# Two conformers ahead of the delta rule's groups, and twelve small copies on another engine

## The chip, the cores and the metric

The kernel runs on one core of one Trainium2 chip. The metric is the device time of one execution in microseconds. The core has TensorE (PE: matrix products into PSUM), VectorE (DVE), ScalarE (ACT), GpSimd (POOL), and SyncE (SP), whose queue issues the DMAs of this kernel. Each engine takes its instructions strictly in the order in which they were put on it.

## The reference, cut to what matters

One layer of a hybrid encoder, for a prompt of 2048 tokens and a decode group of 32 tokens that share all weights. Three mixers read the same normalised input, and their outputs are joined:

```python
hn = rmsnorm(h, W['norm_mix'][i])
proj = hn @ W['w_in'][i]
qkv_pre, z, ba, u5, cc = jnp.split(proj, [OFF_Z, OFF_BA, OFF_S5, OFF_CC], axis=-1)
ya, ... = gdn_mixer(...)        # conv of width 4 on q/k/v, then the chunked delta rule
yb, ... = s5_mixer(u5, ...)     # diagonal state space model, scan over time, GLU
yc, ... = conformer_conv(cc, ...)
mix = jnp.concatenate([ya, yb, yc], axis=-1)
h = h + mix @ W['w_out'][i]
hf = rmsnorm(h, W['norm_ffn'][i])
h = h + (silu(hf @ W['ffn_w1'][i]) * (hf @ W['ffn_w3'][i])) @ W['ffn_w2'][i]
h = h + (p[i] @ W['pe_w'][i]) * sigmoid(h @ W['pe_gate_w'][i])
```

`conformer_conv` is a gate, a causal depthwise convolution of width 31 over 256 channels, a LayerNorm and a swish. It needs nothing but its own columns of the projection and the 30 tokens before. `gdn_mixer` convolves q, k and v over four tokens, and then carries a matrix state from chunk to chunk: block b needs the state that block b-1 leaves. `s5_mixer` carries a state too. All is fp32 at the interface; each large product is made of three products of split operands (high x high, low x high, high x low).

## The kernel before, in words

The tokens are in four blocks of 512 columns (`BLK`; the last block has the 32 decode tokens too, 544 columns in two chunks of 272). Features are on the 128 partitions. Two phases run over the blocks:

- `PhaseA.block(b)`, b = 0 to 3: the projection. `conv` makes one of the 12 column groups of q, k and v: it loads a weight, puts the last three columns of the block before (`tails`, for the decode group `taild`) in front of the tile `raw`, writes the product behind them on VectorE (L615), keeps the new last three columns in `tails`, and then either convolves (blocks 0 and 1) or stores `raw` to DRAM as it is (blocks 2 and 3, `G.raw`, L620). `raw` has two buffers. The small copies are those of lines 609, 611, 616 and 618.
- `PhaseF.block(b)`: output projection `w_out` on the mixers' outputs `mixT[b]` (loaded in L1155, split into `fah` and `fal`), the FFN (`hidden` and `w2`, in groups of four hidden tiles and a last one of two), the gated embedding, the final norm. Products go to PSUM tiles `ps_d` (three buffers, `psD`), and VectorE takes them out: L1173 for w_out, L1218 for w2, L1242 and L1243 for the gates.

Beside them runs the mixers' work that isn't a plain product, written as Python generators ("heads"): `s5_init`, `conformer_block(b)`, `gdn_group` (two per block, and one for the decode group after block 3) and `s5_unit(u)` (two, of two blocks each). A `yield k` gives k steps back. Each call of `dense` counts its columns, and whenever a stage's number of columns is reached (`STAGE`: 9216 in PhaseF's block 0, else 7168), every running generator goes on by one step. So the heads' instructions are emitted in between the dense ones. `first_heads` (s5_init, conformer 0, gdn 0) and `first_s5` run beside PhaseA; `later_heads` starts with PhaseF and makes, in this order, conformer 1, gdn 1, conformer 2, s5 1, gdn 2, conformer 3, gdn 3. Before `PhaseF.block(b)` the heads are emitted at least as far as gdn b.

The order on each engine is then made by a scheduler that works with a simulated time: among the instructions that are ready it takes the one of the lowest priority number. Weight loads, splits and evictions have the class "first"; the heads and the dense matmuls have the class "later", in the order of their emission. An instruction of the heads can thus run long before the place where it was emitted, where an engine is free.

The heads' memory is a stack on the right side of SBUF: `R(name)` opens a pool, and a pool that is opened after another was closed lies in the same place; a tile there waits for the tiles before it that it overlaps (`reuse_waits="tile"`). Conformer 1's pool `cc_1` follows the pool of S5's first unit; gdn 1's pool lies over `cc_1`; conformer 2's over gdn 1's, and so on.

In `conformer_block` the taps are L824 (the first of 31) and L826 (30 more), for two halves of 128 channels: 62 instructions on VectorE for a block. Then come transposes on TensorE (L837), statistics (L840, L841), transposes back (L856) and the swish (L864).

Of the kernel before, what the change touches and what calls it, by code (L numbers as in the profile page):

```python
# [18 lines left out]
BLK = 512  # L19
# [15 lines left out]
def chunks_of(n):  # L35
    c = -(-n // 512)
    w = n // c
    return [(i * w, w) for i in range(c)]


def pieces(c0, cn, hist):

    out = []
    a, b = c0, min(c0 + cn, BLK)
    if a < b:
        out.append((0, hist + a, b - a))
    a, b = max(c0, BLK), c0 + cn
    if a < b:
        out.append((a - c0, hist + BLK + hist + (a - BLK), b - a))
    return out  # L50
# [30 lines left out]
def load_weight(G, src, K, name, key):  # L81


    nc = G.nc
    shp = [P] + (list(K) if isinstance(K, tuple) else [K]) + [P]
    with G.first():
        wr = G.wraw.tile(shp, F32, tag="wr", name=f"wr_{name}")
        nc.sync.dma_start(wr, src)
        wh = G.whi.tile(shp, F32R, tag="wh", name=f"wh_{name}")
        wl = G.wlo.tile(shp, F32R, tag="wl", name=f"wl_{name}")  # L90
        kept = G.low.get((name, key))
        if kept is not None:
            nc.sync.dma_start(wl.bitcast(F32), kept)
        nc.scalar.activation(wh, wr, AF.Copy)  # L94
        if kept is None:

            e = nc.vector if name == "w3" else nc.gpsimd
            e.tensor_tensor(wl, wr, wh.bitcast(F32), op=ALU.subtract)  # L98
            if G.NB > 1:
                kept = G.dd.tile(shp, F32, tag=f"lo_{name}{key}", name=f"lo_{name}{key}")  # L100
                G.low[(name, key)] = kept
                nc.sync.dma_start(kept, wl.bitcast(F32))
    return wh, wl


def dense(G, pool, tag, w, xh, xl, ks, c0, cn, start=True, stop=True, ps=None):

    nc = G.nc
    wh, wl = w
    if ps is None:  # L110
        ps = pool.tile([P, 512], F32, tag=tag, name="ps_d")
    K = len(ks)
    G.step(3 * K * cn)
    with G.later():
        _dense(nc, ps, wh, wl, xh, xl, ks, K, c0, cn, start, stop)
    return ps
# [455 lines left out]
class PhaseA:  # L572
# [27 lines left out]
    def conv(self, m, jj, b, hf, hl, bc, n, last, t0):  # L600

        G, A, wp = self.G, self.A, self.wp
        nc = G.nc
        V = nc.vector
        tails, taild, cw = self.tails, self.taild, self.cw
        w = load_weight(G, A.w_in[m], KD, "qkv", m)
        W = BLK + (3 + TS if last else 0)
        raw = wp.tile([P, W + 3], F32, tag="raw", name="raw")
        nc.gpsimd.tensor_copy(raw[:, 0:3], tails[:, m])
        if last:  # L610
            nc.gpsimd.tensor_copy(raw[:, BLK + 3:BLK + 6], taild[:, m])
        for c0, cn in chunks_of(n):
            p_ = dense(G, G.psD, "pd", w, hf, hl, list(range(KD)), c0, cn)
            for so, do, ln in pieces(c0, cn, 3):
                V.tensor_tensor(raw[:, do:do + ln], p_[:, so:so + ln], bc[:, c0 + so:c0 + so + ln], op=ALU.mult)  # L615
        nc.gpsimd.tensor_copy(tails[:, m], raw[:, BLK:BLK + 3])
        if last:
            nc.gpsimd.tensor_copy(taild[:, m], raw[:, W:W + 3])
        if b in G.raw:
            nc.sync.dma_start(G.sild[b][:, jj], raw)  # L620
            return
        acc = wp.tile([P, W], F32, tag="gacc", name="gacc")
        nc.scalar.activation(acc, raw[:, 0:W], AF.Copy, scale=cw[:, m, 0:1])
        for t in range(1, 4):
            V.scalar_tensor_tensor(acc, raw[:, t:t + W], cw[:, m, t:t + 1], acc, op0=ALU.mult, op1=ALU.add)
        th = wp.tile([P, W], F32, tag="gth", name="gth", bufs=1)
        nc.scalar.activation(th, acc, AF.Tanh)
        V.scalar_tensor_tensor(acc, th, 1.0, acc, op0=ALU.add, op1=ALU.mult)
        nc.sync.dma_start(G.sild[b][:, jj, 0:BLK], acc[:, 0:BLK])
        if last:  # L630
            nc.sync.dma_start(G.sild[b][:, jj, BLK:BLK + TS], acc[:, BLK + 3:W])
# [626 lines left out]
def trunk_kernel(ctx: ExitStack, tc: tile.TileContext, A):  # L1258
    nc = tc.nc
# [51 lines left out]
    NB = G.NB  # L1311
# [60 lines left out]
    R = lambda name, bufs=1: tc.tile_pool(name=name, bufs=bufs, side="right", reuse_waits="tile")  # L1372

    def conf(b, wp):
        return conformer_block(G, A, b, wp, G.psM)
# [13 lines left out]
    def conf_of(b):  # L1389
        with R(f"cc_{b}") as wp:  # L1390
            yield from conf(b, wp)

    def s5_of(u):
        with R(f"s5_{u}") as wp:
            yield from s5_unit(G, A, u, wp, G.psM)

    def gdn_of(b):
        with R(f"gd_{b}", 2) as sp:
            for i in range(2):
                state[0] = yield from gdn_part(b, i, state[0], sp)  # L1400
# [37 lines left out]
    ready = [0]  # L1438

    def later_heads():  # L1440
        for b in range(1, NB):
            yield from conf_of(b)
            if b % G.UB == 0:
                yield from s5_of(b // G.UB)
            yield from gdn_of(b)
            ready[0] = b

    G.start(later_heads())
    for b in range(NB):
        G.flush(lambda: ready[0] >= b)  # L1450
# [117 lines left out]
```

## Time and profile before

| what | value |
|---|---|
| median of three runs | 2888.64 us (2888.06 to 2892.27) |
| the profiled execution | 2888.11 us |
| its span (first to last instruction) | 2886.3 us |
| TensorE busy | 2763.9 us, 96% of the span |
| TensorE weight load busy | 2359.9 us, 82% |
| VectorE busy | 1751.6 us, 61% |
| ScalarE busy | 935.2 us, 32% |
| GpSimd busy | 549.4 us, 19% |
| PhaseF's blocks start at | 682.7, 1230.75, 1779.3 and 2347.25 us |

The start of a block of PhaseF is its first matmul with `wh_out`. In the profile's rows "busy" is the time in which an engine executes; a row with "<-" names in brackets how long the engine was idle before the instruction and what ended the idle time. A row of stretches gives, for each engine, busy time and number of instructions, then TensorE's granted clock (1.00 is full speed), the DMA engines' share and GB/s.

### The profile page before, as it was taken

Reading aid. Unit: us, or ns where it says so; the run is one execution under the profiler, and the core shown is the slowest. Engines: PE = TensorE matmul, PEld = TensorE weight load, DVE = VectorE, ACT = ScalarE, POOL = GpSimd, SP = SyncE. Lnnn points to the kernel's source line nnn. Section 1 sums busy time; section 2 is a strip of 40 time slices with the busy share of each in tenths; the row PEclk is TensorE's granted clock in tenths of the full one; section 3 lists DMA queues with packets and bytes.
Section 4 is the critical chain, followed back from the end, with each engine's and each line's share of the span. In section 5 each row is a group of like instructions: output and inputs, shape, how many; then the busy total and the mean of one; then the engine's idle time right before and its main releaser. Section 6 shows DMA issues by size and latency. Waiting matters only on the chain.

```text
span 2886.3 us, 41015 instructions
## 1 busy us (share of the span) xinstructions
PE 2763.9 (96%) x15300; PEld 2359.9 (82%) x15300; DVE 1751.6 (61%) x3933; ACT 935.2 (32%) x1409; POOL 549.4 (19%) x460
## 2 busy tenths in 40 slices
PE   7899999999999999899999999999999979999997
PEld 5668778898878887688888887778888869999997
DVE  8969765865675847966563755856464733333343
ACT  4243423313422222343422333342332423222232
POOL 5731312234232323421010101000010110000000
PEclk9999999999999999999999999999999979999998
DMA  6578777657654555487665657566565654555553
GB/s 225 170 252 269 248 227 227 199 181 245 206 185 167 190 168 200 152 288 220 216 183 176 187 174 242 187 207 192 172 193 154 197 193 149 174 175 176 175 187 107
DMA packets 278919, 565.32 MB, mean 196 GB/s; under 512 B 67344, under 2 KB 126880, under 8 KB 278576
## 3 DMA queue, kind: packets, MB, share of 16 engines
q1 hardware_dynamic: 278720, 562.70, 60.4%
q8 instruction: 121, 1.98, 0.3%
q14 instruction: 78, 0.64, 0.1%
HBM read 457.76 MB, written 104.25 MB: 195 GB/s over the span
## 4 chain that ended last, share of the span: by engine, by line
PE 64%; DVE 8%; DMA 3%; issue 3%; SPq 1%; ACT 1%; POOL 0%; DVEq 0%; POOLq 0%; ACTq 0%
PE ps_d L122 57%; DVE cacc L826 3%; PE ps_kk L935 1%; PE ps_q L1013 1%; PE ps_z L1026 1%; DVE ct L982 1%; DVE cx L983 1%; DVE hb L1218 1%; DMA xd<-cx 1%; DMA hb<-mixT 1%; PE ps_vn L1069 0%; PE ps_o L1083 0%; PE ps_o L1084 0%; PE ps_s L1076 0%; PE ps_ks L1056 0%
## 5 line engine op out<-in xcount | busy, mean ns | idle before, releaser
L94 ACT ACTIVATE wh_w<-wr_w 128x1024 fp32r<-128x1024 f32 (+1 forms) x272 | 281.3, 1034 | 762.9 <-PE ps_d L122 551.4
L122 PE MATMUL ps_d<-fah,wh_w 128*128 128x512 f32 (+1 forms) x1760 | 379.4, 354 | 7.4 <-DVE fa L1196 2.9
L122 PE MATMUL ps_d<-fal,wh_w 128*128 128x512 f32 (+1 forms) x1760 | 376.5, 353 | 0.0
L122 PE MATMUL ps_d<-fah,wl_w 128*128 128x512 f32 (+1 forms) x1760 | 376.1, 353 | 0.0
L122 PEld LDWEIGHTS ps_d<-fah,wh_w 128*128 128x128 f32 x1760 | 291.1, 189 | 53.6 <-issue 4.0
L122 PEld LDWEIGHTS ps_d<-fal,wh_w 128*128 128x128 f32 x1760 | 291.4, 189 | 43.2
L122 PEld LDWEIGHTS ps_d<-fah,wl_w 128*128 128x128 f32 x1760 | 291.3, 189 | 43.2 <-issue 0.4
L1218 DVE TENSOR_TENSOR hb<-hb,ps_d 128x512 f32<-128x512 f32 (+1 forms) x240 | 139.7, 583 | 167.1 <-PE ps_d L122 166.7
L122 PE MATMUL ps_d<-acth,wh_w 128*128 128x512 f32 (+1 forms) x880 | 210.3, 355 | 9.1 <-DVE hb L1218 7.7
L122 PE MATMUL ps_d<-acth,wl_w 128*128 128x512 f32 (+1 forms) x880 | 210.1, 354 | 0.0
L122 PE MATMUL ps_d<-actl,wh_w 128*128 128x512 f32 (+1 forms) x880 | 208.6, 354 | 0.0
L826 DVE SCALAR_TENSOR_TENSOR cacc<-xc,cc_w,cacc 128x512 f32<-128x512 f32 (+1 forms) x240 | 189.4, 824 | 0.0
L122 PEld LDWEIGHTS ps_d<-acth,wh_w 128*128 128x128 f32 x880 | 148.6, 189 | 34.7 <-DVE hb L1218 6.1
L122 PEld LDWEIGHTS ps_d<-actl,wh_w 128*128 128x128 f32 x880 | 149.4, 189 | 22.2
L122 PEld LDWEIGHTS ps_d<-acth,wl_w 128*128 128x128 f32 x880 | 149.2, 189 | 22.2
L98 POOL TENSOR_TENSOR wl_w<-wr_w,wh_w 128x1024 fp32r<-128x1024 f32 (+1 forms) x46 | 108.2, 2351 | 253.9 <-ACT wh_w L94 226.3
L1201 DVE SCALAR_TENSOR_TENSOR fth<-ps_d,bc 128x512 f32<-128x512 f32 (+1 forms) x110 | 64.8, 589 | 132.0 <-PE ps_d L122 131.3
L1196 DVE TENSOR_TENSOR fa<-ps_d,bc 128x512 f32<-128x512 f32 (+1 forms) x110 | 64.5, 588 | 118.5 <-PE ps_d L122 109.4
L122 PE MATMUL ps_d<-hh,wh_qkv 128*128 128x512 f32 (+1 forms) x480 | 107.2, 365 | 13.8 <-DVE raw L615 13.0
L1204 DVE TENSOR_TENSOR actl<-fa,acth 128x512 fp32r<-128x512 f32 (+1 forms) x110 | 81.3, 739 | 51.3 <-ACT acth L1203 50.9
L1199 DVE SCALAR_TENSOR_TENSOR fa<-fth,fa 128x512 f32<-128x512 f32 (+1 forms) x110 | 73.1, 667 | 58.8 <-ACT fth L1198 58.6
L122 PE MATMUL ps_d<-hh,wl_qkv 128*128 128x512 f32 (+1 forms) x480 | 105.5, 361 | 2.3 <-POOL wl_qkv L98 2.3
(479 smaller groups left out, 4783.3 us busy)
## 6 DMA issues: line engine op xcount, KB each, us to landing
wr_w<-in_w SPq DMA_DIRECT2D x256, 512.0 KB, 4.3
wl_w<-lo_w SPq DMA_DIRECT2D x192, 512.0 KB, 4.0
lo_w<-wl_w SPq DMA_DIRECT2D x64, 512.0 KB, 2.9
wr_qkv<-in_w_in SPq DMA_DIRECT2D x48, 512.0 KB, 4.7
wl_qkv<-lo_qkv SPq DMA_DIRECT2D x36, 512.0 KB, 4.2
wr_out<-in_w_out SPq DMA_DIRECT2D x32, 512.0 KB, 5.2
wr_gate<-in_pe_gate SPq DMA_DIRECT2D x32, 512.0 KB, 4.3
wl_out<-lo_out SPq DMA_DIRECT2D x24, 512.0 KB, 5.9
```

The source lines that it names most:

```text
L94: nc.scalar.activation(wh, wr, AF.Copy)
L98: e.tensor_tensor(wl, wr, wh.bitcast(F32), op=ALU.subtract)
L122: nc.tensor.matmul(ps[:, :cn], a[:, i, :], x(k)[:, c0:c0 + cn], start=start and p_ == 0 and i == 0, stop=stop and p_ == 2 and i == K - 1)
L826: V.scalar_tensor_tensor(acc[:, j], xc[:, j, t:t + W], cn_.w[:, j, t:t + 1], acc[:, j], op0=ALU.mult, op1=ALU.add)
L935: nc.tensor.matmul(kk4[:, h - h0], kq[:, 2 * h, cw], kq[:, 2 * h:2 * h + 2, cw], start=True, stop=True)
L982: V.tensor_tensor(t, cx[:, 0:nq, j:j + 1].to_broadcast(sh), cu[:, j:j + 1, j + 1:].to_broadcast(sh), op=ALU.mult)
L983: V.tensor_tensor(cx[:, 0:nq, j + 1:], cx[:, 0:nq, j + 1:], t, op=ALU.subtract)
L1196: V.tensor_tensor(a, p1[:, :cn], bc[:, cs], op=ALU.mult)
L1199: V.scalar_tensor_tensor(a, th, 1.0, a, op0=ALU.add, op1=ALU.mult)
L1201: V.scalar_tensor_tensor(th, p3[:, :cn], 0.5, bc[:, cs], op0=ALU.mult, op1=ALU.mult)
L1204: V.tensor_tensor(fb[:, cs], a, fa[:, cs].bitcast(F32), op=ALU.subtract)
L1218: V.tensor_tensor(hb[m][:, c0:c0 + cn], hb[m][:, c0:c0 + cn], p_[:, :cn], op=ALU.add)
```

## The change

Two edits. The four copies of `conv` are made on VectorE instead of GpSimd: 12 column groups in four blocks with two copies each, and in the last block two more each, 120 copies of 128x3. And `later_heads` opens the pools of conformers 1 and 2 side by side and makes both conformers first; the rest follows in the same order as before: gdn 1, s5 1, gdn 2, conformer 3, gdn 3.

```diff
         raw = wp.tile([P, W + 3], F32, tag="raw", name="raw")
-        nc.gpsimd.tensor_copy(raw[:, 0:3], tails[:, m])
+        V.tensor_copy(raw[:, 0:3], tails[:, m])
         if last:
-            nc.gpsimd.tensor_copy(raw[:, BLK + 3:BLK + 6], taild[:, m])
+            V.tensor_copy(raw[:, BLK + 3:BLK + 6], taild[:, m])
         ...
-        nc.gpsimd.tensor_copy(tails[:, m], raw[:, BLK:BLK + 3])
+        V.tensor_copy(tails[:, m], raw[:, BLK:BLK + 3])
         if last:
-            nc.gpsimd.tensor_copy(taild[:, m], raw[:, W:W + 3])
+            V.tensor_copy(taild[:, m], raw[:, W:W + 3])
 ...
     def later_heads():
+
+        first = list(range(1, min(3, NB)))
+        with ExitStack() as cx2:
+            wps = [cx2.enter_context(R(f"cc_{b}")) for b in first]
+            for b, wp in zip(first, wps):
+                yield from conf(b, wp)
         for b in range(1, NB):
-            yield from conf_of(b)
+            if b not in first:
+                yield from conf_of(b)
             if b % G.UB == 0:
                 yield from s5_of(b // G.UB)
             yield from gdn_of(b)
```

## The prediction

> **What bounds the kernel now.** I read the page first (engines, slices), then the waits of TensorE by stretches, then the timeline at the four places where it idles, and last the chain of waits there.
>
> ```profile
> PE 2763.9 (96%) x15300; PEld 2359.9 (82%) x15300; DVE 1751.6 (61%) x3933; ACT 935.2 (32%) x1409; POOL 549.4 (19%) x460
> PE   7899999999999999899999999999999979999997
> DVE  8969765865675847966563755856464733333343
> PEclk9999999999999999999999999999999979999998
> ```
>
> TensorE is busy 96% of a span of 2886.3 us; the 122 us that are left lie in few slices: the first two, slice 17 (about 1155 to 1227 us), slice 33 (2309 to 2381) and the last. Only there can a change of order gain. Names: F0 to F3 are the four blocks of PhaseF, "heads" the work of the generator chain. The stretches of F0, F1, F2 and of the gap before F3, with each engine's busy time (PE, PEld, DVE, ACT, POOL) and TensorE's clock:
>
> ```profile
> 682.00:1231.00 549.00, 528.85 (x2495) 429.90 (x2494) 378.61 (x627) 172.28 (x248) 189.85 (x95) 0.99 0.57 191
> 1231.00:1776.00 545.00, 543.68 (x2688) 448.07 (x2686) 317.69 (x768) 189.13 (x275) 59.88 (x46) 1.00 0.64 201
> 1776.00:2316.00 540.00, 528.36 (x2529) 432.30 (x2528) 341.45 (x813) 189.30 (x289) 44.98 (x36) 0.99 0.62 196
> 2316.00:2354.00 38.00, 18.02 (x71) 12.68 (x72) 17.13 (x32) 8.68 (x14) 10.63 (x8) 0.56 0.50 174
> ```
>
> Who TensorE waited for in 1120 to 1210 us (first three rows: total, times, longest), and in 2310 to 2350 (last three):
>
> ```profile
> PE ps_d L122 <- DVE hb L1218: 10.0, 6, 3.0
> PE ps_d L122 <- ACT gth L1241: 3.9, 3, 3.0
> PE ps_d L122 <- ACT wh_w L94: 1.2, 1, 1.2
> ...
> PE ps_ot L1109 <- DVE o L1101: 10.1, 1, 10.1
> PE ps_d L122 <- ACT fah L1134: 5.7, 1, 5.7
> PE ps_vn L1069 <- DMA X<-xd: 4.4, 1, 4.4
> ```
>
> The first group is F0's tail, where w2's last group has only six matmuls to an eviction (L1218) while conformer 2's 62 taps sit between the evictions on VectorE. The second is the end of gdn(3), its short decode part, which F3 waits for. The 240 taps of L826 are four conformers; those of conformer 1 (60 of them, 500 to 660 us) and of conformer 2 (1080 to 1230):
>
> ```profile
> 500.00:660.00 160.00, 42.10 (x60) 0.99 0.61 192
> 1080.00:1230.00 150.00, 58.75 (x60) 0.97 0.52 180
> ```
>
> That is 0.70 us a tap early and 0.98 late. The heads' order, by their marks in the timeline (gdn(1)'s last output, conformer 2's last, s5(1)'s first load, F2's first matmuls (two rows), gdn(3)'s last output, F3's first matmuls):
>
> ```profile
> 1108.89 0.75 DVE L1110 SCALAR_TENSOR_TENSOR zy<-ps_ot,gnw,zy 128x512 f32<-128x512 f32 x1 [4.74 <-DMA zy<-zgd]
> 1237.06 0.68 DVE L864 SCALAR_TENSOR_TENSOR cxn<-cth,cxn 128x512 f32<-128x512 f32 x1
> 1244.37 0.43 SPq L438 DMA_DIRECT2D glu<-in_glu_w  x1
> 1779.32 0.50 PE L122 MATMUL ps_d<-fah,wh_out 128*128 128x512 f32 x1 [3.16 <-ACT fah L1134]
> 1780.59 1.66 PE L122 MATMUL ps_d<-fah,wh_out 128*128 128x512 f32 x3 [0.78 <-ACT fah L1134]
> 2341.55 0.35 DVE L1110 SCALAR_TENSOR_TENSOR zy<-ps_ot,gnw,zy 128x128 f32<-128x128 f32 x1 [0.72 <-PE ps_ot L1109]
> 2347.25 2.94 PE L122 MATMUL ps_d<-fah,wh_out 128*128 128x272 f32 x9 [5.74 <-ACT fah L1134]
> ```
>
> Are the heads late because they are emitted late, or because each step waits for the one before? Counted from the yields, a conformer has 18 steps, gdn(1) 64, s5 48, gdn(2) 80, and gdn(3) with its decode part 108: the end is step 354. F0 emits 112 steps (1,032,192 columns by 9216), F1 and F2 144 each (by 7168). Step 354 stands at step 98 of F2, at 1776 + 98 x 540/144 = 2143 us; it ran at 2341.6. So from s5(1) on the heads are bound by their own latency, and what s5(1) starts earlier the end gains one for one, until F2's dense work is the later of the two. The chain of waits at the end shows it:
>
> ```profile
> 2316.27 1.83 DMA xd<-cx
> 2318.24 1.69 DMA X<-xd
> 2319.97 1.47 PE ps_vn L1069 x8
> ```
>
> **The change part by part.** Durations are from the profiled execution: 2888.11 us, of which 2886.3 are the span; the median of the three runs is 2888.64, so one scale serves.
>
> *Conformer 2 leaves F0's tail.* Its taps, statistics and output move; their number, their DMAs (one load, two stores on SP's queue) stay. The 15.1 us of TensorE's waits above have it as cause, since it is every second instruction on VectorE there; gdn(1)'s last steps now run in this stretch instead and keep a few. Ends 0 and -20 (15.1 and some 5 of reduced clock: 0.97 over 150 us); I take -12.
>
> *It goes to 617 us and on,* behind conformer 1's taps, which ran from 563 to 617 in phase A's last block (its first and last instruction, then the stretch):
>
> ```profile
> 563.17 0.55 DVE L824 TENSOR_SCALAR cacc<-xc,cc_w,cc_b 128x512 f32<-128x512 f32 x1 [0.81 <-DMA xc<-xcd]
> 616.75 0.73 DVE L826 SCALAR_TENSOR_TENSOR cacc<-xc,cc_w,cacc 128x512 f32<-128x512 f32 x1
> ...
> 560.00:682.00 122.00, 119.63 (x968) 117.91 (x967) 80.04 (x197) 26.14 (x44) 32.74 (x49) 0.99 0.60 192
> ```
>
> VectorE is 80.0 of 122 us busy there, with conformer 1 in it; 62 taps at 0.70 are 43 us, so they fill the rest and run on into F0's w_out. Cover for the evictions: three PSUM buffers. No cover for gdn(0): its end is on the path to F0, as these rows show (its last output, the load of it on SP, F0's first matmul):
>
> ```profile
> 674.32 0.75 DVE L1110 SCALAR_TENSOR_TENSOR zy<-ps_ot,gnw,zy 128x512 f32<-128x512 f32 x1
> 677.47 0.84 SPq L1155 DMA_DIRECT2D hb<-mixT  x2
> 682.70 0.74 PE L122 MATMUL ps_d<-fah,wh_out 128*128 128x512 f32 x2 [0.21 <-ACT fah L1134]
> ```
>
> What taps do to such a chain: gdn(0)'s 31 solve steps among conformer 1's taps took 52 us, gdn(2)'s, alone, 22.
>
> ```profile
> L983 DVE TENSOR_TENSOR cx<-cx,ct x31: 153/194/220, 542.3 to 594.6; 128x60 f32<-128x60 f32 x3, 128x28 f32<-128x28 f32 x2, 128x54 f32<-128x54 f32 x2, 128x48 f32<-128x48 f32 x2
> L983 DVE TENSOR_TENSOR cx<-cx,ct x31: 171/211/240, 1486.3 to 1508.1; 128x60 f32<-128x60 f32 x3, 128x28 f32<-128x28 f32 x2, 128x54 f32<-128x54 f32 x2, 128x48 f32<-128x48 f32 x2
> ```
>
> So 30 us over 62 dependent instructions, 0.5 us each. From 617 to 675 gdn(0) has some 20 dependent ones: 10 us, by which F0 starts later. Ends 0 (all taps sink into gaps) and 43 (all ahead); I take +10, near the per-instruction row.
>
> A rule against this: the Trainium skill, GPSIMD Engine Reference, section Specifications, says that GpSimd's SBUF interfaces are shared with VectorE and contend with VectorE instructions of two SBUF inputs, which the taps are. The late taps at 0.98 fit it: GpSimd is 35% busy in F0 (189.85 of 549), 27% in the early stretch (32.74 of 122). If the new place were as bad, F0 would slip by 14 instead of 10 and the sum be 4 worse; conformer 1's 0.70 was measured in the new place itself, so the sum keeps it.
>
> *gdn(1) is emitted 18 steps later,* s5(1) at the same place. A step of F0 is 9216 columns; at full clock 577 matmuls of 272 columns fill 72.2 us:
>
> ```profile
> 2525.50:2597.70 72.20, 72.20 (x577) 72.20 (x576) 24.60 (x56) 18.62 (x29) 0.00 (x0) 1.00 0.55 175
> ```
>
> so a step is 4.2 us and 18 are 76. With the slip, gdn(1) ends at 1109 + 76 + 10 = 1195 instead of 1109; F0 ends at 1231 - 12 + 10 = 1229, 34 us later, so F1 doesn't wait. Behind gdn(1)'s end stand, on SP, F1's eight loads and then s5(1)'s first load: about 12 us, 1207. Before it was 1244, because conformer 2 stood between and held its memory until 1237. The heads are 37 us earlier from here.
>
> *F2's start.* gdn(2) ends 37 us earlier, F1 only 2; the 3.9 us for `fah` at F2's start (3.16 and a second of 0.78) go: -4. Late next is conformer 3, which moves into F1's last gates: it costs there what it cost in F2's w_out, so 0.
>
> *F3's start.* gdn(3) ends at 2341.6 - 37 = 2305. F2's dense work ended at 2316; it ends at 2316 - 12 + 10 - 4 + 4 = 2314, the last 4 for gdn(3)'s matmuls, which now lie inside. Output, load and split after 2305 took 5.7 us (2341.55 to 2347.25), so they are through at 2311. F3 starts near 2315, not 2347. In the sum, apart from the shifts: F3's first 22 matmuls were through at 2354 and need 2.8 us at full clock, so some 35 us lay between F2's and them; 31 of these go. Ends 0 (heads no earlier) and -31. I take -31.
>
> *The copies.* 120 copies of 128x3 leave GpSimd for VectorE. GpSimd's and VectorE's nearest rows, what GpSimd's copies waited for, and what TensorE waited for up to 655 us:
>
> ```profile
> L609 POOL COPY raw<-tails x48: 183/232/2390, 62.3 to 640.3; 128x3 f32<-128x3 f32 x48
> L493 DVE COPY X<-s5x 64x2 f32<-64x2 f32 x16 | 2.6, 161 | 0.2
> ...
> POOL raw L609 <- DMA sild<-raw: 55.2, 19, 5.7
> ...
> PE ps_d L122 <- DVE raw L615: 15.0, 7, 5.8
> PE ps_d L122 <- POOL wl_qkv L98: 2.3, 1, 2.3
> ```
>
> 120 x 0.16 = 19 us of VectorE work over phase A; 24 of them (4 us) in block 0, where VectorE is full (slice 2: 9). Against that, GpSimd's queue no longer stands in front of `wl_qkv`. No row shows a copy waiting on VectorE. Ends -17 (both waits of TensorE go) and +55 (every wait for a buffer moves over and reaches TensorE); I take +3, near block 0's 4.
>
> Sum: -12 + 10 - 4 + 4 - 31 + 3 = -30; 2888.1 - 30 = 2858 us.
>
> **The rivals.** (B) *The heads gain nothing.* If conformer 2 takes its whole old stretch in the new place (1108.9 to 1237.1: 128 us instead of 86), gdn(1) ends at 1237, s5(1) starts as before, F3 starts at gdn(3)'s end as before, and the stalls saved earlier are only waited out there: 2887. For it: it shares VectorE and two PSUM buffers with gdn(0). Against: at F0's start VectorE has room for 18 steps.
>
> (C) *VectorE takes over GpSimd's waits.* VectorE runs in order; a copy that waits for `sild<-raw` (up to 5.7 us) holds the evictions behind it. All 55.2 us on the path: 2858 + 55 = 2913; from 30 us on the change is no gain, from 36 it is slower. Against: the eviction into the same buffer has the same wait, only later, and TensorE has three PSUM buffers.
>
> (D) *Relief.* GpSimd free, block 0's 17 us go, and gdn(0) isn't held up: 2858 - 17 - 3 - 10 = 2828 at best, likelier 2836.
>
> (E) *Half.* The heads come only 15 us earlier: F3 starts at 2332; 2873.
>
> **How the numbers follow.** Forecast 0.52 (2838 to 2875), E 0.07, D 0.10, B 0.14, C 0.17. A measurement of this kernel can tell 0.2%, 5.8 us. Faster 0.52 + 0.07 + 0.10 = 0.69; same 0.14; slower 0.17. Range 2836 to 2894: it takes in B and the beginning of C, leaves out half of D and most of C, under 2 in 10.
>
> **What would show it.** Right: conformer 2's taps near 0.7 us between 600 and 700; the waits on `hb` L1218 in F0's tail under 5 us; s5(1)'s first load near 1207; F3's first matmul within 5 us of F2's last; F0's first matmul near 693. Wrong: s5(1) at 1235 or later (B), TensorE waiting for L615 in blocks 2 and 3 of phase A (C), F1 waiting for `fah` at its start, or conformer 3 among w2's last evictions in F1 as conformer 2 was in F0.

## Result and profile after: 1.8% slower

The changed kernel takes 2941.82 us (median of 4 runs, 2940.84 to 2943.91) against 2889.18 us of the kernel before, run beside it: ratio 1.0182, 95% interval 1.0167 to 1.0198. Forecast were 2858 us and a range of 2836 to 2894. The profiled execution has a span of 2941.7 us. Its page, in the lines that the prediction read first (busy time; TensorE's busy tenths in 40 slices of 73.5 us; its granted clock):

```profile
PE 2775.5 (94%) x15300; PEld 2370.6 (81%) x15300; DVE 1756.1 (60%) x4053; ACT 938.8 (32%) x1409; POOL 494.6 (17%) x340
PE   7789899996799999999999999999999979999997
PEclk9899999996899999999999999999999979999998
```

VectorE and GpSimd did what the diff says: 120 instructions moved, VectorE 4.5 us more, GpSimd 54.8 less. TensorE has a hole that wasn't there (slices 10 and 11 from the left: 6 and 7, clock 0.6 and 0.8), its dip in F0's tail (slice 17 before) is gone, and the dip ahead of F3 has stayed. The stretches of the changed kernel, cut at the first matmul of F0, F1, F2 and F3, columns as in the prediction (length, then busy time and count of PE, PEld, DVE, ACT, POOL, then clock, DMA share, GB/s):

```profile
0.00:761.40 761.40, 650.83 (x3514) 538.80 (x3514) 575.61 (x1503) 237.91 (x376) 183.94 (x159) 0.92 0.64 203
761.40:1285.00 523.60, 520.68 (x2482) 427.70 (x2483) 323.93 (x554) 165.80 (x232) 181.19 (x87) 1.00 0.58 193
1285.00:1832.00 547.00, 544.93 (x2668) 449.70 (x2668) 311.10 (x750) 189.65 (x276) 57.52 (x43) 0.99 0.65 203
1832.00:2401.00 569.00, 540.88 (x2577) 439.39 (x2575) 352.29 (x838) 190.42 (x291) 54.85 (x41) 0.97 0.60 189
2401.00:2941.70 540.70, 518.18 (x4062) 515.00 (x4062) 193.16 (x410) 155.03 (x236) 17.08 (x12) 0.97 0.51 168
```

And of the kernel before, the first stretch:

```profile
0.00:683.00 683.00, 634.55 (x3487) 528.59 (x3488) 508.78 (x1291) 226.55 (x359) 231.35 (x267) 0.97 0.69 220
```

Before, the other four were 548, 548, 568 and 539 us long (the starts in the table of the profile before). So the account is short: phase A is 78 us longer (62 of them idle TensorE; 16 more busy, with 27 matmul records more, conformer 2's transposes, and a mean clock of 0.92 against 0.97), F0 is 24 us shorter, the rest is as it was. What F0 waited for, in the timeline of the changed kernel (gdn(0)'s last output, F0's first loads of it, F0's first matmul; then gdn(1)'s last output, s5(1)'s first load, gdn(3)'s last output, F3's first matmul):

```profile
754.47 0.75 DVE L1110 SCALAR_TENSOR_TENSOR zy<-ps_ot,gnw,zy 128x512 f32<-128x512 f32 x1 [5.52 <-DMA zy<-zgd]
757.89 2.23 SPq L1155 DMA_DIRECT2D hb<-mixT  x5
761.44 4.25 PE L122 MATMUL ps_d<-fah,wh_out 128*128 128x512 f32 x9 [12.43 <-ACT fah L1134]
...
1254.39 0.75 DVE L1110 SCALAR_TENSOR_TENSOR zy<-ps_ot,gnw,zy 128x512 f32<-128x512 f32 x1 [0.34 <-DMA zy<-zgd]
1266.89 0.33 SPq L438 DMA_DIRECT2D glu<-in_glu_w  x1
...
2393.98 0.34 DVE L1110 SCALAR_TENSOR_TENSOR zy<-ps_ot,gnw,zy 128x128 f32<-128x128 f32 x1
2401.49 1.78 PE L122 MATMUL ps_d<-fah,wh_out 128*128 128x272 f32 x6 [13.33 <-ACT fah L1134]
```

F0 waits for gdn(0), whose last output comes at 754 instead of 674. The solve of its second half, which took 52 us before (542.3 to 594.6), in the changed kernel:

```profile
L983 DVE TENSOR_TENSOR cx<-cx,ct x31: 176/207/224, 581.7 to 702.5; 128x60 f32<-128x60 f32 x3, 128x28 f32<-128x28 f32 x2, 128x54 f32<-128x54 f32 x2, 128x48 f32<-128x48 f32 x2
```

It begins 39 us late and takes 121 us. Each instruction is nearly as short as before (mean 207 ns against 194); what is new stands between the steps. Two questions follow: which edit makes gdn(0) late, and why nothing is won before F3.

### The profile page after: what moved, and what is told of

It is laid out like the page before. It is cut to its first block, busy times and chain, and to the rows that moved or that the text cites. A ratio compares the mean times of both kernels' runs of the same rounds, so it can differ in the third digit from the quotient of the medians.

```text
span 2941.7 us, 40924 instructions
## 1 busy us (share of the span) xinstructions
PE 2775.5 (94%) x15300; PEld 2370.6 (81%) x15300; DVE 1756.1 (60%) x4053; ACT 938.8 (32%) x1409; POOL 494.6 (17%) x340
## 4 chain that ended last, share of the span: by engine, by line
PE 73%; DVE 14%; DMA 7%; issue 3%; SPq 2%; ACT 1%; POOL 1%; DVEq 0%; ACTq 0%; POOLq 0%
PE ps_d L122 65%; DVE cacc L826 3%; DVE gacc L625 1%; DMA wl_qkv<-lo_qkv 1%; PE ps_kk L935 1%; PE ps_q L1013 1%; PE ps_z L1026 1%; DMA hb<-mixT 1%; DMA mixT<-zy 1%; DVE kq L891 0%; PE ps_o L1083 0%; DVE hb L1253 0%; PE ps_ks L1056 0%; PE ps_o L1084 0%; PE ps_s L1076 0%
## 5 line engine op out<-in xcount | busy, mean ns | idle before, releaser
L1218 DVE TENSOR_TENSOR hb<-hb,ps_d 128x512 f32<-128x512 f32 (+1 forms) x240 | 139.8, 584 | 190.7 <-PE ps_d L122 190.3
L826 DVE SCALAR_TENSOR_TENSOR cacc<-xc,cc_w,cacc 128x512 f32<-128x512 f32 (+1 forms) x240 | 184.8, 800 | 0.0
L98 POOL TENSOR_TENSOR wl_w<-wr_w,wh_w 128x1024 fp32r<-128x1024 f32 (+1 forms) x46 | 107.8, 2344 | 254.0 <-ACT wh_w L94 236.8
L1204 DVE TENSOR_TENSOR actl<-fa,acth 128x512 fp32r<-128x512 f32 (+1 forms) x110 | 87.9, 799 | 44.1 <-ACT acth L1203 43.9
```

What stands on the lines that cost most here:

```text
L826: V.scalar_tensor_tensor(acc[:, j], xc[:, j, t:t + W], cn_.w[:, j, t:t + 1], acc[:, j], op0=ALU.mult, op1=ALU.add)
L1204: V.tensor_tensor(fb[:, cs], a, fa[:, cs].bitcast(F32), op=ALU.subtract)
L1218: V.tensor_tensor(hb[m][:, c0:c0 + cn], hb[m][:, c0:c0 + cn], p_[:, :cn], op=ALU.add)
```

## The experiments

Each kernel was timed beside the kernel before on the same chip. One kernel's runs lie up to 19 us apart, so the ratios decide; a stretch comes from one profiled execution each, and a difference of a few us in it says nothing. "Setup" is `s5_init`'s part on TensorE (L340 to L368: eight transposes with each of two inputs, and 32 small products), the first work of the heads that TensorE does; S5's unit 0, conformer 0 and gdn(0) come behind it.

### Each edit alone

`copies_only` has the diff's first part, `order_only` its second.

> The kernel before with the copies of the short convolution's history on VectorE and nothing else. Theory 1 (the order alone costs the 52 us): 2888 +- 6 us, conformer 0's first tap near 226 us as before, gdn(0)'s last output near 674. Theory 2 (the copies alone make the heads 36 us late in phase A, and the order only passes this on): conformer 0's first tap near 252, gdn(0)'s second solve from about 580, its last output near 705, F0 starts 25 to 35 us late, 2905 to 2920 us. Theory 3 (both are needed: the copies bring the lateness, which costs nothing until conformer 2's taps are ready beside the late solve): the marks of theory 2 in phase A, and a time under 2915.

> The kernel before with conformers 1 and 2 first and nothing else. Theory 1: gdn(0)'s second solve starts near 542 us as before, conformer 2's taps stand between its steps from about 560 on and it takes 100 us or more instead of 52; F0's first matmul near 740 to 760; 2925 to 2945 us. Theory 2: the solve is through before conformer 2's taps are ready, F0's first matmul by 700, 2855 to 2880 us, as forecast. Theory 3: in between, F0's first matmul 700 to 740, 2880 to 2925.

Measured: copies alone 2933.44 us, ratio 1.0146 (1.0127 to 1.0165); order alone 2883.74 us, 0.9983 (0.9971 to 0.9995). Theory 1 falls: the order alone costs nothing, the copies cost nearly all. Of theory 2 the early marks came (251 and 580 us), but the copies alone cost more than it allowed (F0 40 us late, a time above 2920); with the order alone F0 starts at 705, the in-between of theory 3. The stretches of the kernel with the order alone up to F2's end:

```profile
0.00:705.00 705.00, 638.15 (x3514) 529.45 (x3514) 551.94 (x1383) 236.96 (x376) 252.86 (x278) 0.96 0.68 219
705.00:1227.00 522.00, 519.49 (x2480) 427.85 (x2481) 323.16 (x554) 165.78 (x233) 180.41 (x87) 1.00 0.58 194
1227.00:1776.00 549.00, 545.80 (x2669) 449.63 (x2668) 311.97 (x750) 189.75 (x277) 57.28 (x44) 0.99 0.64 203
1776.00:2344.00 568.00, 540.71 (x2579) 440.95 (x2578) 353.33 (x840) 191.26 (x292) 52.91 (x41) 0.97 0.59 190
```

The order gains 26 us in F0 and loses 22 ahead of it. With the copies alone (first two stretches) it is 40 us ahead of F0 and nothing behind:

```profile
0.00:723.00 723.00, 641.60 (x3498) 533.12 (x3498) 526.96 (x1426) 233.25 (x368) 181.40 (x154) 0.94 0.66 212
723.00:1269.00 546.00, 528.42 (x2478) 431.08 (x2479) 375.14 (x610) 167.87 (x238) 183.52 (x88) 0.98 0.55 186
```

Both together give 761.4: the order costs 38 us ahead of F0 when the copies have made gdn(0) late, 22 when they haven't. The same row of gdn(0)'s solve, with the order alone:

```profile
L983 DVE TENSOR_TENSOR cx<-cx,ct x31: 153/196/222, 541.5 to 619.7; 128x60 f32<-128x60 f32 x3, 128x28 f32<-128x28 f32 x2, 128x54 f32<-128x54 f32 x2, 128x48 f32<-128x48 f32 x2
```

78 us, between 52 and 121: conformer 2's taps start at 566.10, not at 617 as the forecast had it, so they stand among the steps, and all the more when the solve begins at 582.

### Where the taps hold gdn(0)

`hold_output` and `hold_solve` are the order alone with conformer 2's VectorE instructions queued behind one of gdn(0)'s:

```diff
+    def held(gen):
+        while True:
+            with tc.issue_after(G.zy_last):  # gdn(0)'s last zy (L1110); hold_solve: G.cx_last, its last solve step (L983)
+                try:
+                    y = next(gen)
+                except StopIteration:
+                    return
+            yield y
...
-                yield from conf(b, wp)
+                yield from conf(b, wp) if b == 1 else held(conf(b, wp))
```

> Conformers 1 and 2 first, copies on GpSimd, and conformer 2's VectorE instructions queued behind gdn(0)'s last output (L1110). If the fault lies only in conformer 2's taps standing between gdn(0)'s steps (theories 1 and 3): gdn(0)'s second solve takes about 52 us as before, F0's first matmul 680 to 690 us, the waits for hb L1218 in F0's tail under 5 us, gdn(1)'s last output near 1190, s5(1)'s first load near 1205, gdn(3)'s last output near 2305, 2840 to 2865 us. If the forecast's other terms were wrong too (conformer 2's steps cost F0 as much at its start as at its end): 2875 to 2895 us with F0's first matmul in place.

> As the one before, but conformer 2's VectorE instructions are queued behind the last step of gdn(0)'s second solve (L983) alone: the place that the forecast gave them. If the forecast's price is right (0.5 us for each of some 20 dependent instructions): F0's first matmul 10 us later than with the hold behind the output, 690 to 697 us, and a time 8 to 12 us longer. If each dependent instruction waits for all the taps that are ready (in the changed kernel 62 of them cost 99 us more than the 22 of an undisturbed solve, 1.6 us each): F0's first matmul 25 to 40 us later, and a time 20 to 40 us longer.

Measured: 2887.26 us, 0.9995 (0.9977 to 1.0013), and 2889.76 us, 1.0006 (0.9992 to 1.0021). Held behind the output, F0 starts at 686.9, but is 547.6 us long again. Held behind the solve, F0 starts at 701.3, 14 us later, and is 523.6 long. So of the first kernel's two cases it is the second that came: gdn(0) is through in time, and F0 pays for conformer 2 at its start as it did at its end. Of the second kernel's two prices (10 us, or 25 to 40) neither came, 14 is nearer the first; and F0 gets it back, so the time is only 2.5 us longer. Conformer 2 costs about the same at each of three places: at F0's end (548.0 us in the kernel before), at its start (547.6), or in phase A's end (F0 begins 19 to 22 us late). The order gives back what it gains.

### Why the copies cost 40 us

The first mark that differs between the kernels is the setup on TensorE: its first transpose, its last product, and conformer 0's first tap, which waits for the setup's memory. Before:

```profile
141.89 0.82 PE L346 MATMUL ps_pt<-ident,Pre 128*128 128x128 f32 x6
196.99 0.39 PE L360 MATMUL ps_kg<-nHim,Bim 64*16 64x128 f32 x2
225.97 0.99 DVE L824 TENSOR_SCALAR cacc<-xc,cc_w,cc_b 128x512 f32<-128x512 f32 x2
```

With the copies alone:

```profile
173.72 1.03 PE L346 MATMUL ps_pt<-ident,Pre 128*128 128x128 f32 x8
226.41 0.38 PE L360 MATMUL ps_kg<-nHim,Bim 64*16 64x128 f32 x2
250.87 1.00 DVE L824 TENSOR_SCALAR cacc<-xc,cc_w,cc_b 128x512 f32<-128x512 f32 x2
```

None of these rows has a bracket, so TensorE did not wait just before them: the transposes stand further back in its queue, behind 536 matmuls instead of 440 (the last product behind 744 instead of 625, counted in the kernels' queues). The schedule was made anew around the moved copies. To tell that place from the copies themselves, four kernels emit the setup in the class ahead of the dense work, where it stands behind some 360 matmuls; `early_init` is the kernel before with this, the others have it with the copies, the order, and both:

```diff
     yield 2
+    with G.heads():                       # the rest indented under it, to L368
     C.PT = []
```

> The kernel before, with the transposes and the small products of the S5's setup (L340 to L368) emitted in the priority class ahead of the dense work, so that they stand behind 362 matmuls in TensorE's queue and not behind 440; nothing else. First transpose near 117 us instead of 142, conformer 0's first tap near 200 instead of 226, gdn(0)'s last output near 650 instead of 674. F0 is then started by phase A's last dense work (680 us) and not by gdn(0): 2880 to 2890 us, no change to 0.3% faster.

> The copies on VectorE with the S5's setup emitted early (behind 359 matmuls; with the copies alone it stood behind 536, and its first transpose ran at 174 us instead of 142). Theory 1 (the copies cost nothing on VectorE; their 37 us are the place that the heads' first instructions got in TensorE's queue): conformer 0's first tap within 5 us of the run with early setup alone, gdn(0) through before 680, and a time within 6 us of that run, 2880 to 2892. Theory 2 (VectorE's in-order queue takes over the waits for the raw buffers and holds all heads): conformer 0 early, but gdn(0)'s last output 20 us or more later than in the run with early setup alone, and 2900 us or more.

> Conformers 1 and 2 first, copies on GpSimd, S5's setup early. With the order alone gdn(0)'s last output came at 698 us instead of 674 and F0's first matmul at 705 instead of 683, while F0 itself took 522 us instead of 548. If the lateness of gdn(0) is all that ate the gain: gdn(0)'s last output near 675, F0's first matmul 683 to 690, F0 still 522 to 528 us long, and 2860 to 2870 us. If the conformers start earlier as well and again run between gdn(0)'s steps: F0's first matmul near 700 and 2878 to 2888 us.

> The changed kernel (both edits) with the S5's setup early. Theory 1: as conformers 1 and 2 first with early setup, within 6 us: 2860 to 2870 us, F0's first matmul under 692 instead of 761. Theory 2: at least 20 us more than conformers 1 and 2 first with early setup, F0's first matmul at 705 or later.

Measured:

| kernel | median us, ratio to before | conformer 0's first tap | gdn(0)'s last output | F0 starts |
|---|---|---|---|---|
| early_init | 2900.87, 1.0045 (1.0025 to 1.0064) | 180 | 685 | 694 |
| copies_early_init | 2915.96, 1.0101 (1.0074 to 1.0128) | 185 | 698 | 707 |
| order_early_init | 2895.44, 1.0026 (1.0015 to 1.0038) | 181 | 712 | 719 |
| both_early_init | 2915.64, 1.0095 (1.0066 to 1.0124) | 187 | 725 | 732 |

A miss in one way: `early_init` itself was to take 2880 to 2890 us, and none of the other three came into its first range. The 46 us that conformer 0 wins are gone at its end (325 us, against 328 before), and gdn(0) is through 11 us later than before. Here a lead at the head of this chain isn't carried to its end. But the copies' price falls from 46 to 15 us, that of both edits from 53 to 15, both counted against `early_init`; against `order_early_init` the copies cost 20, as theory 2 said. Then the other direction: `late_init` moves no copy and only queues the setup behind 536 matmuls, `copies_in` moves only L609's copies, `copies_out` only L616's. `order_fast_emit` belongs to the next part.

```diff
+    last = [i for i in nc.cur_bb.bb.instructions if i.engine == nc.tensor.engine][-149]
+    with G.tc.issue_after(last):           # late_init: L340 to L368 indented under it
```

> The kernel before, copies on GpSimd, order as before; only the transposes and small products of the S5's setup (L340 to L368) are queued later on TensorE, behind 536 matmuls, where the copies' kernel has them (the kernel before: 440). Theory 1 (what the copies cost comes from this place in the queue): first transpose near 172 us, conformer 0's first tap near 250, gdn(0)'s last output 700 to 717, F0's first matmul 705 to 723, 2908 to 2933 us. Theory 2 (the copies' own time and waits on VectorE): conformer 0 late, but gdn(0) makes it up as it gave up the lead with the early setup (46 us earlier at conformer 0's first tap, 11 us later at gdn(0)'s last output): gdn(0)'s last output 674 to 685, 2885 to 2900 us.

> The kernel before with only the copies from the history into the buffer (raw<-tails, L609; they wait for the buffer) on VectorE; those back (L616) stay on GpSimd. The setup then stands behind 536 matmuls, as with all copies moved. Theory 1 (place) and theory 2 (waits for the buffer on VectorE) both expect most of the cost: 2915 to 2935 us. A third, that only the number of instructions on VectorE counts, expects about half: 2905 to 2912.

> The kernel before with only the copies back into the history (tails<-raw, L616; behind the eviction on the same engine, no wait of their own) on VectorE. The setup stands behind 464 matmuls instead of 440. Theory 1 and theory 2 expect nothing or little: conformer 0's first tap 226 to 233, 2885 to 2897 us. The third, that the number of instructions counts: 2905 to 2912.

Measured: 2920.82 us, 1.0119 (1.0090 to 1.0149); 2927.53, 1.0136 (1.0119 to 1.0153); 2923.35, 1.0129 (1.0106 to 1.0152). The same three marks of the kernel in which only the setup was queued later:

```profile
176.04 1.04 PE L348 MATMUL ps_pt<-ident,Pre 128*128 128x128 f32 x8
219.96 0.38 PE L362 MATMUL ps_kg<-nHim,Bim 64*16 64x128 f32 x2
243.52 1.00 DVE L826 TENSOR_SCALAR cacc<-xc,cc_w,cc_b 128x512 f32<-128x512 f32 x2 [2.83 <-DMA xc<-xcd]
```

gdn(0)'s last output is then at 709 and F0 at 715.8, both in theory 1's ranges, as is the time: this alone costs 34 us with all copies on GpSimd. Each half of the copies costs nearly as much as all of them (40 and 36 of 46 us), so their number is not the price. In `copies_out`, for which none of the three theories had 2923 us, the first transpose is at 151 but the last product at 223, and conformer 0 starts at 248 all the same: the last product stands as far back in the queue as in `late_init` (771 matmul records of the trace lie ahead of it in both, 661 in the kernel before).

Last, the copies with the setup put back (`copies_same_place`: transposes behind 442 and 480 matmuls, products behind 561 to 602), the whole change so (`both_same_place`), and each half so. The edit is `early_init`'s with two `issue_after` in it, as in `late_init`.

> All copies on VectorE, and the S5's setup put back where the kernel before has it in TensorE's queue: transposes behind 442 and 480 matmuls (before: 440 to 551), the small products behind 561 (before: 552). Theory 1 (the place is the cause): first transpose near 143 us, conformer 0's first tap 224 to 232, gdn(0)'s last output 674 to 685, 2885 to 2898 us. Theory 2 (the copies on VectorE cost time themselves, as the 15 us between the two kernels with early setup say): conformer 0 early, gdn(0)'s last output 690 or later, 2900 to 2915 us.

> The whole change, with the S5's setup put back to that place. Theory 1: as conformers 1 and 2 first without the copies, F0's first matmul near 705 instead of 761, 2880 to 2893 us. Theory 2: 15 us or more above that, 2897 to 2912 us, F0's first matmul 718 or later.

> Only the copies into the buffer (raw<-tails) on VectorE, with the S5's setup at its place of before (441, 480, 561 matmuls ahead). If the 20 us that are left with all copies moved are VectorE's waits for the raw buffer (DMA sild<-raw): about the same waits, 25 to 40 us in total from 225 to 692 us, gdn(0)'s last output near 692, 2900 to 2912 us. If it is the number of copies on VectorE: 2893 to 2900 us.

> Only the copies back into the history (tails<-raw) on VectorE, with the S5's setup at its place of before. If the rest is the waits for the buffer: none of them on VectorE, gdn(0)'s last output 672 to 680, 2882 to 2893 us (against 2923 with the setup late). If it is the number of copies on VectorE: 2893 to 2900 us; and if the setup's place was not the cause of this half's 36 us, 2910 us or more.

| kernel | median us, ratio to before | the same without the place restored | conformer 0's first tap | gdn(0)'s last output | F0 starts |
|---|---|---|---|---|---|
| copies_same_place | 2906.62, 1.0070 (1.0046 to 1.0094) | 2933.44 | 225 | 692 | 700 |
| both_same_place | 2901.86, 1.0050 (1.0034 to 1.0065) | 2941.82 | 225 | 718 | 725 |
| copies_in_same_place | 2905.83, 1.0061 (1.0040 to 1.0082) | 2927.53 | 220 | 680 | 700 |
| copies_out_same_place | 2909.50, 1.0075 (1.0050 to 1.0100) | 2923.35 | 229 | 696 | 705 |

Putting the setup back takes away 27 of the copies' 46 us, 40 of the change's 53, and 22 of 40 and 14 of 36 for the two halves. The order then costs 25 us ahead of F0 (725 against 700), near the 22 that it costs alone. But 15 to 22 us are left in every kernel: the first two times lie in theory 2's ranges, the third in the range of the waits for the buffer, and the fourth just under the 2910 us from which on the place was not to be that half's cause. With all copies moved, the longest of VectorE's waits from 225 to 692 us are these (total, times, longest):

```profile
DVE raw L611 <- DMA sild<-raw: 33.7, 16, 6.3
DVE raw L617 <- PE ps_d L122: 10.8, 7, 4.2
```

So VectorE does take over part of the waits for the buffer that GpSimd had (55.2 us of them in the kernel before), as rival C said. But with the half that has no such wait of its own the list begins

```profile
DVE raw L617 <- PE ps_d L122: 22.1, 12, 4.2
DVE hl L78 <- ACT hh L77: 14.1, 6, 4.5
```

and the time is no better. So this wait can't be the whole of the rest. Nor is gdn(0) everywhere the way that the rest takes: in `copies_in_same_place` it is through at 680, and TensorE works at phase A's own products without a wait from there to F0's start at 700. What the rest is stays open. It may be the schedule again: putting the setup into another class moved the kernel before by 12 us with no copy touched (`early_init`), all four kernels of this table have that class too, and no run has it with the setup at its old place and the copies on GpSimd. A third buffer for `raw`, which would take the waits away, wasn't tried.

### Why F3 starts no earlier

With the order alone the marks that the forecast named are there (gdn(0)'s last output, F0's first matmul; gdn(1)'s last output, s5(1)'s first load, F1's first matmul; gdn(3)'s last output, F3's first matmul):

```profile
698.06 0.75 DVE L1110 SCALAR_TENSOR_TENSOR zy<-ps_ot,gnw,zy 128x512 f32<-128x512 f32 x1 [5.21 <-DMA zy<-zgd]
705.00 7.32 PE L122 MATMUL ps_d<-fah,wh_out 128*128 128x512 f32 x22 [9.07 <-ACT fah L1134]
...
1196.74 0.75 DVE L1110 SCALAR_TENSOR_TENSOR zy<-ps_ot,gnw,zy 128x512 f32<-128x512 f32 x1 [0.68 <-DMA zy<-zgd]
1208.17 0.47 SPq L438 DMA_DIRECT2D glu<-in_glu_w  x1
1227.04 2.00 PE L122 MATMUL ps_d<-fah,wh_out 128*128 128x512 f32 x8
...
2336.14 0.34 DVE L1110 SCALAR_TENSOR_TENSOR zy<-ps_ot,gnw,zy 128x128 f32<-128x128 f32 x1
2343.71 1.79 PE L122 MATMUL ps_d<-fah,wh_out 128*128 128x272 f32 x6 [13.41 <-ACT fah L1134]
```

s5(1) starts 36 us earlier than before, gdn(3) ends 5 us earlier. The prediction took the heads there to be bound by their own latency and so to pass the lead on. Two other pacers were tried: the rate of emission (`order_fast_emit`: `STAGE` 6144 instead of 7168 in F1 and F2) and the heads' low class (`heads_ahead`, `order_heads_ahead`):

```diff
-        with at("later"):
+        with at(G.hclass):                # "heads" (ahead of the dense work) from F1 on
             c[1] = next(c[0], 0)
```

> Conformers 1 and 2 first, copies on GpSimd, and in F1 and F2 a step of the heads is emitted for every 6144 columns of dense work instead of 7168 (F0 stays at 9216). With the order alone s5(1)'s first load came 36 us earlier than before, gdn(3)'s last output only 6 us earlier. If the heads are paced there by where they are emitted: gdn(2)'s last output 40 to 75 us before the 1757 of the order alone, gdn(3)'s last output before 2310, F3's first matmul within 5 us of F2's last, 2850 to 2868 us. If their own latency paces them, as the forecast assumed: the marks within 8 us of the order alone, 2876 to 2890 us.

> The kernel before, with the heads in the priority class ahead of the dense work from F1 on, so that in each engine's queue they stand where they are ready and not where dense work leaves room. If their low class paces them: gdn(2)'s last output 30 us or more before 1771, gdn(3)'s before 2310, F3's first matmul within 5 us of F2's last, and 2855 to 2870 us. If the chain's own waits pace them (transfers, TensorE to VectorE and back): gdn(3)'s last output within 10 us of 2342, 2880 to 2895 us.

> Conformers 1 and 2 first, copies on GpSimd, heads ahead of the dense work from F1 on. If the low class took the lead of s5(1) away: s5(1)'s first load near 1208, gdn(2)'s last output by 1730, gdn(3)'s by 2300, F3 without a stall, 2848 to 2862 us. If not: within 6 us of the order alone, 2878 to 2890 us.

Measured: 2885.52 us, 0.9989 (0.9976 to 1.0003); 2888.85, 1.0007 (0.9993 to 1.0022); 2882.88, 0.9983 (0.9973 to 0.9993). All three times lie in the range named for the case that neither emission nor class is the pacer. None moves gdn(3)'s end by more than 7 us against the same order without it: 2343 and 2337 against 2336, and 2344 against 2342 in the order before. So of the pacers tried none is left but the chain's own waits, as the forecast assumed, and yet the lead is lost. Where it goes is read from rows: s5(1)'s four groups of products start at 1258, 1293, 1323 and 1356 us before; with the order alone the third and fourth start at 1302 and 1339, the first two at

```profile
1219.90 1.12 PE L468 MATMUL ps_v<-ug,c_PT 128*64 128x132 f32 x16 [1.32 <-DMA c_PT<-s5PTre]
1270.41 1.12 PE L468 MATMUL ps_v<-ug,c_PT 128*64 128x132 f32 x16
```

The first step takes 50 us instead of 35. The second group's loads now fall into F1's first stretch and stand in SP's queue between F0's output and F1's weights:

```profile
1251.16 0.90 SPq L449 DMA_DIRECT2D ug<-us  x2
1252.80 0.34 SPq L93 DMA_DIRECT2D wl_out<-lo_out  x1
1253.97 5.67 SPq L1254 DMA_DIRECT2D out_yT<-hb  x8
1259.73 0.94 SPq L88 DMA_DIRECT2D wr_w<-in_w  x1
1260.72 1.40 SPq L449 DMA_DIRECT2D ug<-us  x1
```

The lead is 38 us at the first group, 22 at the second, 17 at the fourth and at conformer 3's first tap (1772.94 against 1790), and 5 at gdn(3)'s end. That this queue is the cause of the first loss is read, not tried.

## Point by point

- *Conformer 2 out of F0's tail, -12.* Right in kind, but only half of it: F0 is 26 us shorter with the order alone and 24 in the changed kernel, more than the end of -20. Of the waits for `hb` L1218 there (10.0 us before) none is listed any more; TensorE's busy time falls by 9 us, with 15 matmul records fewer and a clock of 1.00 against 0.99.
- *gdn(0) held up, +10.* This is the step that failed for the order: 22 us alone, 38 behind the copies. The price was made for 20 instructions behind the solve, from taps that begin at 617; they began at 566, among the solve's 31 steps. At the place that the prediction meant (`hold_solve`) it was 14 us more than held behind the output. Even there F0 starts 19 us later than before, not 10. The upper end of 43 held 22 and 38.
- *gdn(1) 18 steps later, s5(1) 37 us earlier.* Right with the order alone, 1196.7 and 1208.2 for 1195 and 1207, but partly by luck: F0 began 22 us late, not 10, so the 18 steps took 66 us, not 76, and the two errors cancel. In the changed kernel both come 58 us later, with F0.
- *F2's start, -4.* Hardly there: TensorE's wait for `fah` is 2.5 us with the order alone, 3.9 before, and F1 is 549 us long, 548 before.
- *F3's start, -31.* This step failed: "what s5(1) starts earlier the end gains one for one". Of 36 us 5 were left at gdn(3)'s end, and the stretch from F2's start to F3's is 568 us before and after (569 in the changed kernel). Rival B's 2887 is near the 2883.7 of the order alone, though by another way than it said: gdn(1) took no longer than forecast and s5(1) started early. Rival E has the sign right, but its 15 us were 5.
- *The copies, +3.* The largest miss: 46 us by the medians, 40 in the profiled stretch. The ends (-17 and +55) held it; the choice near 4 us of VectorE's time did not. This is the step that failed for the copies: the sum counted their own time and waits and took every other queue as it was. What decided most of it was a third thing: the order on TensorE was made anew, and the heads' first work came to stand 96 matmuls further back. 27 of the 46 us go with that place; the place alone, with no copy moved, costs 34. The rest is open.
- *Rival C (VectorE takes over GpSimd's waits, 2913 us).* Its wait is there (33.7 us in `copies_same_place`, 19.4 in the changed kernel), but not its path: TensorE's waits for the eviction into `raw` up to 692 us are 14.9 us in the changed kernel, 15.0 before, and only 0.2 of them come after 340 us. The half of the copies without the wait costs as much. That its +55 lies near the copies' 46 is luck.
- *Rival D (relief).* Not there: besides those 14.9 us, TensorE's wait for `wl_qkv` grew from 2.3 to 6.0.
- *Taps at 0.70 early and 0.98 late.* Held: 86.01 us for the 120 of conformers 1 and 2 with the order alone (0.72), 0.76 in the changed kernel (91.30 for 120), and 0.94 where `hold_output` puts conformer 2 into F0's start. What makes the late ones late is read in the last section.

The sum as measured, order alone -26 + 22 = -4, copies +40, and 16 more where the order's taps meet a solve that the copies have made late, is +52 (the medians differ by 53 us, the profiled spans by 55). The order alone is the best kernel of these: its interval leaves out 1, but at 0.9983 it stays under the 0.2% that the prediction counted as a change.

## What to carry to other kernels

Where a scheduler fixes each engine's queue ahead of time, an edit of 0.16 us instructions on one engine can move work on another: compare the first mark that differs between the traces, pin the suspect to its old place and, alone, to the new one. In these chains, which share in-order queues with other work, lateness was passed on and a lead mostly wasn't (36 us at s5(1) came to 5 at the end), so take a gain at the end of a chain only at the price of the links in between. Conformer 2 cost much the same at each of the three places tried: look for a place where the engine is idle and nobody waits behind it.

## What was not expected of the hardware

The taps' time goes with the place, but not by how busy GpSimd is. With the order alone the taps of conformers 1 and 2 lie in 560 to 706 us, with conformer 2 held behind gdn(0) its own lie in 678 to 870; the stretches of these two kernels, one row each, and then conformer 2's taps (L826) of the second alone:

```profile
560.00:706.00 146.00, 126.48 (x998) 121.12 (x997) 126.18 (x284) 37.10 (x64) 54.13 (x60) 0.94 0.57 190
```

```profile
678.00:870.00 192.00, 176.17 (x788) 143.19 (x788) 144.33 (x186) 62.26 (x87) 69.72 (x35) 0.96 0.57 196
```

```profile
678.00:870.00 192.00, 56.48 (x60) 0.96 0.57 196
```

GpSimd is busy 37% of the first (54.13 of 146) and 36% of the second (69.72 of 192), and a tap takes 0.72 and 0.94 us. The same taps one by one (shortest, median and longest in ns):

```profile
L826 DVE SCALAR_TENSOR_TENSOR cacc<-xc,cc_w,cacc x120: 709/734/2944, 564.2 to 669.4; 128x512 f32<-128x512 f32 x120
L826 DVE SCALAR_TENSOR_TENSOR cacc<-xc,cc_w,cacc x60: 710/739/2895, 680.5 to 763.3; 128x512 f32<-128x512 f32 x60
```

The median is the same; a few long ones make the mean. One of them in `hold_output`, the tap after it, and what GpSimd does meanwhile:

```profile
714.86 2.85 POOL L98 TENSOR_TENSOR wl_out<-wr_out,wh_out 128x1024 fp32r<-128x1024 f32 x1
715.71 2.54 DVE L826 SCALAR_TENSOR_TENSOR cacc<-xc,cc_w,cacc 128x512 f32<-128x512 f32 x1
718.78 0.74 DVE L826 SCALAR_TENSOR_TENSOR cacc<-xc,cc_w,cacc 128x512 f32<-128x512 f32 x1
```

GpSimd's instruction ends at 717.71, the tap at 718.25. Every tap longer than 1 us is of this kind: 1 of the 120 with the order alone, 3 of 120 in the changed kernel, 9 of these 60, and 14 of conformer 2's 60 in the kernel before (1080 to 1230 us). Each starts while a GpSimd TENSOR_TENSOR of 512 or 1024 columns with two inputs runs (the splits of weights and activations, L98 and L1136) and ends 0.54 to 0.56 us after it. One tap starts well inside such an instruction and is short all the same (0.74 us, at 752.69 in `hold_output`); there it is GpSimd's that takes 3.91 us. The taps beside GpSimd's copies of three columns take 0.73 to 0.74 us, as those beside nothing do. The Trainium skill, GPSIMD Engine Reference, section Specifications, has GpSimd's SBUF interfaces shared with VectorE and in contention with instructions of two SBUF inputs. These traces agree, and they say how much: a tap that starts during such an instruction is done only 0.55 us after its end. So what counts here is which GpSimd instructions run beside the taps, not GpSimd's share of busy time. That is read from four traces; no run moved those splits.
